# Low half of each weight tile from ACT and an accumulating DMA in place of a DVE subtraction (one Trainium2 core, two-layer encoder trunk)

## Chip, cores and metric

One core of one Trainium2 chip. The metric is device time in microseconds (us) of one execution of the whole program; lower is better. Below, PE is TensorE (matmuls), PEld its weight loads, DVE is VectorE, ACT is ScalarE, POOL is GpSimd and SP is SyncE, which here only issues DMAs.

## What is computed

The reference is a two-layer trunk on one sequence of 512 tokens with 1024 features, all in float32. Cut to what matters:

```python
for l in range(DEPTH):                       # DEPTH = 2
    h = rms_norm(x, norm1_g[l])
    za, xb, q, k, v, g = jnp.split(h @ w_in[l], splits, axis=-1)
    ya = spatial_gating(jax.nn.gelu(za), ...)   # A: gMLP gating
    yb = multiscale_pool(xb, ...)               # B: trailing mean pooling
    yc = retention(q, k, v, g, ...)             # C: retention, 8 heads
    x = x + jnp.concatenate([ya, yb, yc], axis=-1) @ w_out[l]
    x = x + conv_ffn(rms_norm(x, norm2_g[l]), w_up[l], ..., w_down[l])   # D_FF = 2816
return rms_norm(x, final_g)
```

## The kernel before, in words

Every large matmul is made to float32 accuracy from three matmuls on float32r operands, a rounded form of float32. An operand a is split into a high half (a rounded to float32r) and a low half (a minus that high half, rounded again), and a product is hi·hi + hi·lo + lo·hi. `mm3` (lines 210 to 214) issues the three for one 128x128 piece of a weight: line 212 (weight hi, activation hi), 213 (weight hi, activation lo), 214 (weight lo, activation hi). So the low half of a weight is first needed by the third matmul.

All weights lie in memory as 192 tiles of 128 partitions by 1024 float32 (512 KB each), 96 a layer, in the order of use. The class `Weights` (lines 54 to 95) brings them in. `first` makes tiles 0 to 3 in halves, interleaved with the loads of x; the change doesn't touch it. The other 188 come from `_emit` (lines 80 to 89): SP issues the load into a raw tile `wr` (line 83), ACT rounds it into the high half `wh` (line 86), DVE subtracts `wh` from `wr` into the low half `wl` (line 87). Each of the three kinds has five buffers. `get(s)` (line 91) is called just before the matmuls of tile s and emits up to tile s + 3 (LOOK = 3). A raw buffer is free for the next load when its readers are done; a `wh` or `wl` buffer is free when the matmuls of its tile are done.

A layer runs in stages. Mixing (lines 246 to 582): the projection v (4 tiles), then the list MIX (lines 43 to 46), with 18 tiles of projections among attention-like work (`scores`, `ymix`), pooling, gating; then the output projection o (8 tiles). In step `q` (lines 321 to 336) POOL issues four SBUF-to-SBUF DMAs of 128 KB that copy half tiles `qs` across partitions, and `scores` (line 353) reads them. Then the FFN in two halves (lines 584 to 629): 22 tiles of up projections, each followed by a short chain on DVE and ACT (lines 604 to 616), then 11 tiles of down projections. That is 22 + 8 + 66 = 96 tiles a layer. The last down projection is laid out by `finish` (line 633) in token halves so that the final norm overlaps it.

Nothing orders the engines by hand: a tile framework works out the waits (semaphores) and plans the order of each engine's queue ahead of time. Each engine then runs its queue strictly in order. The planned order isn't the order of the code. POOL's queue holds a few small memsets, the table loads and the `qs` copies.

Of the kernel before, what the change touches and what calls it, by code (L numbers as in the profile page):

```python
# [10 lines left out]
F32 = mybir.dt.float32  # L11
F32R = mybir.dt.float32r
AF = mybir.ActivationFunctionType
ALU = mybir.AluOpType
# [39 lines left out]
class Weights:  # L54
# [25 lines left out]
    def _emit(self, s):  # L80
        nc = self.nc
        src = self.raw_pool.tile([P, KT, P], F32, tag="raw", name=f"wr{s}")
        nc.sync.dma_start(out=src, in_=self.w[s].rearrange("p (k c) -> p k c", k=KT))
        hi = self.hi_pool.tile([P, KT, P], F32R, tag="hi", name=f"wh{s}")
        lo = self.lo_pool.tile([P, KT, P], F32R, tag="lo", name=f"wl{s}")
        nc.scalar.copy(hi, src)  # L86
        nc.vector.tensor_tensor(out=lo, in0=src, in1=hi.bitcast(F32), op=ALU.subtract)  # L87
        self.slots[s] = (hi, lo)
        self.slots.pop(s - LOOK - 2, None)

# [741 lines left out]
```

## Time and profile before

| what | value |
|---|---|
| time before, median of 2 runs | 1140.86 us (1140.46 and 1141.26) |
| span of the profiled execution, first to last instruction | 1139.3 us |
| what lies around the span, by those two runs | 1.2 to 2.0 us |
| PE busy | 1125.2 us (99%) |
| DVE busy | 746.4 us (66%) |
| ACT busy | 525.1 us (46%) |
| POOL busy | 27.5 us (2%) |
| granted TensorE clock, mean | 0.998 |

The profiled execution has no stopwatch time of its own besides its span, so the two timed runs say what lies around it. A profile line of a group reads: code line, engine, operation, output tile <- input tiles, shapes, count, then busy time in us and mean ns of one, then the engine's idle time before them and what ended it. `xN` is a count. A name ending in q (SPq, ACTq) is the engine's queue, where it waits or issues. PE's matmuls are pipelined: one is listed with 0.39 us but the next starts 0.23 us later.

### The profile page before, as it was taken

How to read it: one execution, taken by the hardware profiler on the slowest of the kernel's cores; microseconds unless marked ns; L12 is line 12 of the kernel's file. 1: busy time of each engine (PE TensorE's matmuls, PEld its weight loads, DVE VectorE, ACT ScalarE, POOL GpSimd, SP SyncE). 2: the span in 40 equal slices, each digit the busy share in tenths (PEclk: the TensorE clock that was granted, in tenths of full speed). 3: DMA queues.
4: the chain of work that ended last, by engine and by line, in shares of the span. 5: the costliest groups of instructions: out<-in, count | busy, mean ns of one | idle time of the engine just before them, and what ended most of it. 6: DMA issues, size and time to landing. Idle time of an engine off the chain costs nothing.

```text
span 1139.3 us, 13715 instructions
## 1 busy us (share of the span) xinstructions
PE 1125.2 (99%) x5378; PEld 941.7 (83%) x5378; DVE 746.4 (66%) x1103; ACT 525.1 (46%) x731; POOL 27.5 (2%) x71
## 2 busy tenths in 40 slices
PE   8999999999999999999999999999999999999997
PEld 6888888888888888888888898888888888888886
DVE  6898676576763377764448877666777435777534
ACT  7577745444431244444327785534444213444420
POOL 2010000000000000000001000000000000000000
PEclk9999999999999999999999999999999999999999
DMA  9433222233223222233224322222232223322202
GB/s 326 146 111 93 75 75 96 90 102 102 93 93 101 103 93 93 97 105 113 93 93 123 100 74 71 78 93 93 96 107 94 93 96 106 95 93 93 93 1 74
DMA packets 33361, 112.83 MB, mean 99 GB/s; under 512 B 4320, under 2 KB 4496, under 8 KB 33296
## 3 DMA queue, kind: packets, MB, share of 16 engines
q1 hardware_dynamic: 29952, 103.82, 27.1%
q0 software_dynamic: 2480, 6.87, 2.3%
q10 hardware_dynamic: 864, 1.26, 0.3%
q8 instruction: 42, 0.69, 0.2%
q14 instruction: 23, 0.19, 0.0%
HBM read 105.64 MB, written 2.10 MB: 95 GB/s over the span
## 4 chain that ended last, share of the span: by engine, by line
PE 99%; DVE 0%; DMA 0%; ACT 0%; issue 0%; DVEq 0%; SPq 0%; ACTq 0%
PE up L214 14%; PE up L212 14%; PE up L213 14%; PE dn L214 5%; PE dn L213 5%; PE dn L212 5%; PE o L212 3%; PE o L214 3%; PE o L213 3%; PE fd L212 2%; PE fd L213 2%; PE fd L214 2%; PE v L241 1%; PE v L242 1%; PE v L243 1%; PE k L213 1%
## 5 line engine op out<-in xcount | busy, mean ns | idle before, releaser
L86 ACT CAST wh<-wr 128x1024 fp32r<-128x1024 f32 x188 | 197.7, 1052 | 291.7 <-PE dn L213 104.2
L87 DVE TENSOR_TENSOR wl<-wr,wh 128x1024 fp32r<-128x1024 f32 x188 | 229.8, 1223 | 106.0 <-ACT wh L86 103.1
L610 DVE SCALAR_TENSOR_TENSOR cc<-uu,vecs,cc 128x511 f32<-128x511 f32 (+1 forms) x176 | 131.4, 748 | 5.4 <-ACT cc L606 2.3
L606 ACT ACTIVATE cc<-uu,vecs 128x512 f32<-128x512 f32 x88 | 71.5, 815 | 7.9 <-DVE uu L604 7.7
L614 ACT ACTIVATE cc<-cc 128x512 f32<-128x512 f32 x44 | 27.8, 632 | 79.0 <-DVE cc L610 79.0
L604 DVE TENSOR_TENSOR uu<-up,n_1bc 128x512 f32<-128x512 f32 x44 | 30.2, 688 | 40.9 <-PE up L214 40.9
L604 DVE TENSOR_TENSOR uu<-up,n_0bc 128x512 f32<-128x512 f32 x44 | 30.2, 688 | 40.9 <-PE up L214 40.9
L626 DVE TENSOR_TENSOR x<-x,dn 128x512 f32<-128x512 f32 x24 | 16.5, 687 | 40.9 <-PE dn L214 40.9
L212 PE MATMUL up<-n_0h,wh 128*128 128x512 f32 x88 | 34.7, 394 | 0.0
L213 PE MATMUL up<-n_0l,wh 128*128 128x512 f32 x88 | 34.3, 390 | 0.0
L214 PE MATMUL up<-n_1h,wl 128*128 128x512 f32 x88 | 34.3, 390 | 0.0
L212 PE MATMUL up<-n_1h,wh 128*128 128x512 f32 x88 | 34.3, 390 | 0.0
L212 PE MATMUL up<-n_3h,wh 128*128 128x512 f32 x88 | 34.3, 390 | 0.0
L214 PE MATMUL up<-n_5h,wl 128*128 128x512 f32 x88 | 34.3, 390 | 0.0
L214 PE MATMUL up<-n_2h,wl 128*128 128x512 f32 x88 | 34.3, 390 | 0.0
L212 PE MATMUL up<-n_7h,wh 128*128 128x512 f32 x88 | 34.3, 390 | 0.0
L213 PE MATMUL up<-n_4l,wh 128*128 128x512 f32 x88 | 34.3, 390 | 0.0
L213 PE MATMUL up<-n_6l,wh 128*128 128x512 f32 x88 | 34.3, 390 | 0.0
L213 PE MATMUL up<-n_5l,wh 128*128 128x512 f32 x88 | 34.3, 390 | 0.0
L214 PE MATMUL up<-n_6h,wl 128*128 128x512 f32 x88 | 34.3, 390 | 0.0
L214 PE MATMUL up<-n_3h,wl 128*128 128x512 f32 x88 | 34.3, 390 | 0.0
L212 PE MATMUL up<-n_4h,wh 128*128 128x512 f32 x88 | 34.3, 390 | 0.0
(959 smaller groups left out, 3058.3 us busy)
## 6 DMA issues: line engine op xcount, KB each, us to landing
wr<-in_wflat_dram SPq DMA_DIRECT2D x188, 512.0 KB, 3.5
wr<-in_wflat_dram SPq DMA_DIRECT2D x8, 256.0 KB, 7.3
x<-in_xT_dram SPq DMA_DIRECT2D x8, 256.0 KB, 7.8
qs_0h<-qs_0h POOLq DMA_DIRECT2D x8, 128.0 KB, 2.3
qs_1h<-qs_1h POOLq DMA_DIRECT2D x8, 128.0 KB, 3.7
qs_0l<-qs_0l POOLq DMA_DIRECT2D x8, 128.0 KB, 3.4
qs_1l<-qs_1l POOLq DMA_DIRECT2D x8, 128.0 KB, 3.8
out_dram<-fin ACTq DMA_DIRECT2D x4, 256.0 KB, 2.2
```

The costliest lines, as they stand in the source:

```text
L86: nc.scalar.copy(hi, src)
L87: nc.vector.tensor_tensor(out=lo, in0=src, in1=hi.bitcast(F32), op=ALU.subtract)
L212: nc.tensor.matmul(ps, hi[:, k, :], xh, start=first, stop=False)
L213: nc.tensor.matmul(ps, hi[:, k, :], xl, start=False, stop=False)
L214: nc.tensor.matmul(ps, lo[:, k, :], xh, start=False, stop=last)
L241: nc.tensor.matmul(o, hs[k][:, bs], hi[:, kk, :], start=k == 0 and b % pack == 0, stop=False)
L242: nc.tensor.matmul(o, hs[k][:, bs], lo[:, kk, :], start=False, stop=False)
L604: nc.vector.tensor_tensor(out=u, in0=ps, in1=nm.bc, op=ALU.mult)
L606: nc.scalar.activation(out=c, in_=u, func=AF.Identity, scale=w[2], bias=vecs[:, vc + C_CB + t : vc + C_CB + t + 1])
L610: nc.vector.scalar_tensor_tensor(out=c[:, d:], in0=u[:, : T - d], scalar=w[2 - d], in1=c[:, d:], op0=ALU.mult, op1=ALU.add)
L614: nc.scalar.activation(out=c, in_=c, func=AF.Silu)
L626: nc.vector.tensor_tensor(out=X[m], in0=X[m], in1=ps, op=ALU.add)
```

## The change

In `_emit` the subtraction on DVE goes. ACT writes the raw tile times -1, rounded to float32r, into the low tile: that is the negated high half. Then a DMA issued by POOL adds the raw tile to it in place (it reads `wr` and `wl` and writes `wl`, all in SBUF). `wl` is then raw minus high, as before.

```diff
@@ Weights._emit
         nc.scalar.copy(hi, src)
-        nc.vector.tensor_tensor(out=lo, in0=src, in1=hi.bitcast(F32), op=ALU.subtract)
+        nc.scalar.activation(out=lo, in_=src, func=AF.Copy, scale=-1.0)
+        nc.gpsimd.dma_start(out=lo, in_=src, accum_op=ALU.add)
         self.slots[s] = (hi, lo)
```

## Rows read from the trace of the kernel before

**Rows 1.** The page's head and busy times of the whole span.
```profile
span 1139.3 us, 13715 instructions
PE 1125.2 (99%) x5378; PEld 941.7 (83%) x5378; DVE 746.4 (66%) x1103; ACT 525.1 (46%) x731; POOL 27.5 (2%) x71
```

**Rows 2.** The chain that ended last, by engine.
```profile
PE 99%; DVE 0%; DMA 0%; ACT 0%; issue 0%; DVEq 0%; SPq 0%; ACTq 0%
```

**Rows 3.** Waits of PE, the two longest: total us, times, longest.
```profile
PE v L241 <- ACT n_0h L176: 5.6, 1, 5.6
PE frb L689 <- DVE fr1r L162: 1.3, 1, 1.3
```

**Rows 4.** Groups of instructions, the two that make the halves.
```profile
L86 ACT CAST wh<-wr 128x1024 fp32r<-128x1024 f32 x188 | 197.7, 1052 | 291.7 <-PE dn L213 104.2 <-PE up L213 66.8 <-PE o L213 39.8
L87 DVE TENSOR_TENSOR wl<-wr,wh 128x1024 fp32r<-128x1024 f32 x188 | 229.8, 1223 | 106.0 <-ACT wh L86 103.1
```

**Rows 5.** Stretches: PE, PEld, DVE, ACT, POOL busy, granted clock, DMA share, GB/s.
```profile
24.00:160.00 136.00, 136.00 (x770) 115.87 (x769) 115.22 (x218) 91.70 (x150) 11.05 (x28) 1.00 0.34 109
...
100.00:130.00 30.00, 30.00 (x195) 27.15 (x194) 22.71 (x49) 25.76 (x46) 2.06 (x4) 1.00 0.29 89
...
206.00:328.00 122.00, 122.00 (x548) 101.32 (x547) 86.26 (x113) 55.45 (x69) 0.00 (x0) 1.00 0.29 96
```

**Rows 6.** PE in order of time, start and length in us: tile starts, FFN.
```profile
300.91 0.39 PE L212 MATMUL up<-n_0h,wh 128*128 128x512 f32 x1
...
306.35 0.39 PE L212 MATMUL up<-n_0h,wh 128*128 128x512 f32 x1
...
328.56 0.39 PE L214 MATMUL dn<-G_0h,wl 128*128 128x512 f32 x1
```

**Rows 7.** ACT in order of time, the same stretch of the FFN.
```profile
304.74 0.63 ACT L614 ACTIVATE cc<-cc 128x512 f32<-128x512 f32 x1 [1.99 <-DVE cc L610]
306.32 1.06 ACT L86 CAST wh<-wr 128x1024 fp32r<-128x1024 f32 x1 [0.95 <-PE up L213]
307.28 0.81 ACT L606 ACTIVATE cc<-uu,vecs 128x512 f32<-128x512 f32 x1
```

**Rows 8.** DVE in order of time, the subtraction that belongs to that cast.
```profile
307.41 1.23 DVE L87 TENSOR_TENSOR wl<-wr,wh 128x1024 fp32r<-128x1024 f32 x1 [0.17 <-ACT wh L86]
```

**Rows 9.** DMA queues (packets, MB, share of 16 engines) and issues (median us to landing).
```profile
q1 hardware_dynamic: 29952, 103.82, 27.1%
q0 software_dynamic: 2480, 6.87, 2.3%
...
wr<-in_wflat_dram SPq DMA_DIRECT2D x188, 512.0 KB, 3.5
...
qs_1l<-qs_1l POOLq DMA_DIRECT2D x8, 128.0 KB, 3.8
...
dmt<-in_dmask_dram POOLq DMA_DIRECT2D x1, 512.0 KB, 7.4
```

**Rows 10.** POOL in order of time: issues at the start and in mixing.
```profile
2.86 0.53 POOL L139 DMA_DIRECT2D dmt<-in_dmask_dram  x1
3.38 0.54 POOL L141 DMA_DIRECT2D dect<-in_vdec_dram  x1
...
65.28 0.52 POOL L335 DMA_DIRECT2D qs_1l<-qs_1l  x1 [0.37 <-issue]
```

**Rows 11.** Waits of SP's queue, the longest.
```profile
SPq L83 <- DVE wl L87: 944.7, 176, 14.1
```

**Rows 12.** ACT in order of time: a table load; the first tile that `_emit` makes.
```profile
1.67 1.28 ACT L75 ACT_TABLE_LOAD   x1 [1.67 <-PEq L820]
...
21.63 1.05 ACT L86 CAST wh<-wr 128x1024 fp32r<-128x1024 f32 x1 [0.18 <-DMA wr<-in_wflat_dram]
```

**Rows 13.** PE in order of time: first low half from `_emit`; second pair's scores.
```profile
31.26 0.39 PE L214 MATMUL q<-n_0h,wl 128*128 128x512 f32 x1
...
73.72 0.39 PE L361 MATMUL sc<-qs_0h,ks 128*128 128x512 f32 x1
```

## The prediction

> **What bounds the kernel now.** I read the page's head first: PE is busy for 1125.2 of 1139.3 us, DVE for 66%, ACT for 46% [rows 1]. The chain that ended last is PE for 99% of the span [rows 2]. The waits of PE say what is left to win: 5.6 us once, for the first activation, and 1.3 us at the very end; between the two PE waits for nothing [rows 3]. The stretches confirm it: in mixing (24 to 160 us) and in the up projections (206 to 328 us) PE is busy all the time at a granted clock of 1.00, which is the 2.4 GHz level [rows 5]. So the kernel is bound by the number of matmuls. An engine that gets lighter gives nothing by itself, and the question is only whether the new way of making the low half is ever late. I therefore looked for how early the low half is made today, and for what the new steps share with others.
>
> **How early it is today.** A tile's 24 matmuls take 306.35 - 300.91 = 5.44 us in the FFN [rows 6]. The cast at 306.32 waited for PE to give back a buffer (the releaser is PE's line 213) [rows 7]; with five buffers this is the tile used four tiles later, at 306.35 + 4 x 5.44 = 328.11, and its low half is first read at 328.56 [rows 6]. The subtraction ends at 307.41 + 1.23 = 308.64 [rows 8]. So the low half lies ready for 19.9 us. It is the five buffers that set this, not the speed of the maker.
>
> **What is removed.** 188 subtractions of 1.223 us, 229.8 us of DVE [rows 4]. They lie beside PE's work and PE never waits for them [rows 3], so their going is worth 0. DVE falls from 746 to 517 us of busy time.
>
> **What is added on ACT.** 188 passes over 128x1024. The trace has no such pass with a factor; the nearest row is the cast of the same tile, 1.052 us [rows 4]. Below I take that as the floor too (the same elements), above the 0.81 us for 128x512 with two vector operands [rows 7], twice: 1.62. I take 1.05, since a constant factor brings no operand from memory. ACT rises to 525 + 188 x 1.05 = 722 us (63%). In the up projections ACT is busy for 55.45 of 122 us, 2.47 us a tile [rows 5]; 2.47 + 1.05 = 3.52 of 5.44, so there it is hidden with room, at the upper price too (4.09). Mixing is tighter: 91.7 of 136 us, with 22 tiles 23 more, 115 (84%), while DVE goes from 115.2 to about 88 [rows 5]; the two change places. The tightest stretch is 100 to 130 us: ACT is busy for 25.76 of 30 us, and with its four tiles it reaches 29.96. Nothing covers an ACT that has no idle time left. From below the cost is 0 (PE had no wait beside a DVE at 85%); from above it is all four passes in each of two layers, 8.4 us. I take one pass a layer, 2.1 us, because those four low halves need not be early and can stand behind more urgent work.
>
> **What is added on POOL and the DMA engines.** 188 issues. POOL issued a DMA of the same 512 KB (dmt) in 0.53 us and the next 0.52 us after it began [rows 10]: 0.53 of 5.44 us, on an engine busy for 2%. Nothing there.
>
> The transfer itself isn't in this trace: no DMA adds. The loads' queue took 27.1% of 16 engines over 1139.3 us for 103.82 MB, that is 4940 engine-us, or 195 ns for 4096 bytes, one partition's row; POOL's queue by the same sum 250 ns [rows 9]. An engine has 8 of a tile's 128 rows, so a load occupies it for 8 x 0.195 = 1.56 us of 5.44, a share of 0.29, which is the share that the stretch shows [rows 5]. An adding row reads two rows and writes one. Below it costs one copy (195 ns, reads and write overlapped), above three in a row (585 ns). I take two, 390 ns, as the middle: two rows must be read through the same engine. A tile then occupies each engine for 3.12 us, with the load 4.68 of 5.44 us, a share of 0.86. It fits. At one copy the share is 0.57; at three it is 6.24 us and doesn't fit (the second rival).
>
> The Trainium skill, page "Collectives: The Full Stack", section "The bandwidth ceiling: the fold count and why AG ≠ RS ≠ AR", says that the adding unit in a DMA engine costs nothing by itself and that a sum runs at half a copy's rate because both sources are read through one ring, with 62.28 against 32.35 GB/s measured. By that price, an estimate, the row costs 1.93 copies, 376 ns, and the share is 0.84. No row here shows an adding DMA.
>
> **Is it late?** From the tile's cast the new path is 1.05 (cast), 1.05 (negation), 0.53 (issue) and the landing. A plain load lands 3.5 us after its issue [rows 9], of which 1.56 are its rows; with 3.12 in their place that is 5.1 us. Together 7.7 us after 306.32, at 314.0, against 328.56: 14.5 us to spare. With the 7.4 us of dmt, the longest 512 KB landing from POOL, it is 12.2. In the FFN and in o the cost is 0. SP's loads change what they wait for: today for the subtraction (944.7 us in 176 waits) [rows 11], then for the adding DMA's landing. A raw buffer comes back some 5 us later, and its next load must land (3.5 us) before the cast five tiles (27.2 us) on: 27.2 - 7.7 - 3.5 leaves 16 us. Also 0.
>
> The one early place without much room is tile 4: cast at 21.63 to 22.68 [rows 12], negation to 23.73 if it stands next, landing 5.6 us later at 29.4; PE reads it at 31.26 [rows 13]. With a landing of 7.4 us in place of 5.1 it comes at 31.7, and behind one more pass of ACT about 1 us later: at most 1.5 us late. I take 0.
>
> **The sum.** 1139.3 (span) + 0 (FFN, o) + 2.1 (mixing) + 0 (start) = 1141.4, and about 1.6 around the span by the two timed runs (1.2 to 2.0): **1143 us**. Its own range is 1138 to 1152 (nothing; all 8.4 in mixing and 1.5 at the start).
>
> **Rivals.**
>
> *POOL's queue delays the copies that scores wait for* (slower). The adding DMAs share POOL's queue with the qs copies. The last copy of the second pair is issued at 65.28 [rows 10], lands 3.8 us later by the median [rows 9], at 69.1, and PE reads that pair at 73.72 [rows 13]: 4.6 us to spare. Two adding DMAs ahead of the copies cost 2 x 3.12 = 6.2 us, 1.6 late; at three copies a row 9.4, 4.8 late. With 8 such sets, 13 to 38 us, in the middle 26: 1139.3 + 26 + 1.6 = 1167. It decides from two adding DMAs ahead. Against it: mixing makes one tile in 6.2 us (136 / 22), so two ahead are rare, and POOL's order is planned ahead, with these transfers in view.
>
> *The DMA engines become the bound* (slower). It decides from a row of (5.44 - 1.56) / 8 = 485 ns on, 2.5 copies. At three copies a tile takes 6.24 us, 0.80 more, for the 148 tiles of o and FFN 118 us, less some 17 us of room used up once a layer: 1139.3 + 84 + 1.6 = 1225; at four copies far more. For it: 0.86 is not far from 1, and POOL's rows cost 250, not 195 ns. Against it: two reads alone make two copies.
>
> *POOL takes the next adding DMA only when the last has landed* (slower). At 7.4 us a tile, 1.96 over, 148 times, less 34: 1397. Against it: at the start POOL issued one after the other in half a microsecond while each landed in some 7 us [rows 9, 10].
>
> *The ACT copy needs another function table* (slower). The pass is an ACTIVATE between Silu and Identity. Two table loads a tile, of 1.28 us [rows 12], would make 2.47 + 1.05 + 2.56 = 6.08 us on ACT, 0.64 over 5.44, in 88 up tiles: 1139.3 + 56 + 1.6 = 1197. Against it: Identity (line 606) and Silu (line 614) take turns without a load between [rows 7]. The Trainium skill, page "ScalarE: Activation LUTs", section "Table sets: the hidden batching unit", says that copy is in every set; by it the rival's price is 0, and the trace agrees for Identity.
>
> *Faster by over 2%.* PE's two longest waits are 6.9 us together [rows 3], 0.6%. Only a tighter matmul could do it, and nothing here points to one.
>
> **How the numbers follow.** About 2% can be told from no change here: 1118.0 and 1163.7. Forecast 0.71, POOL's queue 0.08 (a third of it inside 2%), DMA bound 0.14, waiting for landings 0.04, table 0.02, faster 0.01. So faster 0.01, same 0.74, slower 0.25. The range 1138 to 1180 holds the forecast and the first rival, 0.79.
>
> **What would show it.** Right: PE's only waits are those of rows 3 and a few below 2 us in mixing; DVE near 517, ACT near 722 us; the negation near 1.05 us; POOL's queue with 188 x 128 more row packets at 300 to 450 ns, and DMA share near 0.85 in the up projections; landings of 5 to 8 us. Wrong: PE waiting for `wl` in the FFN with DMA share near 1 (second rival) or below it with issues far apart (third); PE waiting for `sc` behind late qs copies (first); table loads on ACT in the FFN (fourth).

## The result, and the profile after

The changed kernel takes 1148.76 us (median of two runs, 1148.54 and 1148.97) against 1140.86; the ratio on record is 1.0067, with a 95% interval of 1.0049 to 1.0086. It is slower by 7.9 us, inside the 2% and inside the range, and 5.8 us above the forecast of 1143. The profiled execution took 1148.54 us with a span of 1146.8, so 1.7 us lie around the span.

After the change a line number from 88 on stands one higher than in the code before: L87 is the negation on ACT, L88 the adding DMA, L213 to L215 are `mm3`. First the page's head and the busy times of the changed kernel, which answer to [rows 1]:

```profile
span 1146.8 us, 14169 instructions
...
PE 1130.0 (99%) x5378; PEld 941.4 (82%) x5378; DVE 534.4 (47%) x915; ACT 693.1 (60%) x919; POOL 192.8 (17%) x259
```

PE still has 5378 matmuls, yet is busy for 4.8 us more; the first experiment shows where. DVE and ACT have changed places. ACT has exactly 188 instructions more. The chain that ended last, by engine, which was PE for 99% [rows 2]:

```profile
PE 90%; ACT 4%; DMA 3%; DVE 2%; issue 1%; ACTq 0%; DVEq 0%; POOLq 0%; SPq 0%
```

The path now leaves PE at some places and runs through ACT, a DMA and DVE. The groups that make the halves (line, engine, operation, count | busy us, mean ns of one | idle time before, and what ended it):

```profile
L86 ACT CAST wh<-wr 128x1024 fp32r<-128x1024 f32 x188 | 197.4, 1050 | 188.3 <-issue 84.5
L88 POOL DMA_DIRECT2D wl<-wr x188 | 164.6, 876 | 868.6 <-ACT wl L87 815.9
L87 ACT ACTIVATE wl<-wr 128x1024 fp32r<-128x1024 f32 x188 | 197.8, 1053 | 12.3 <-PE v L243 12.3
```

The negation costs what the cast costs. POOL's issue of an adding DMA takes 876 ns. The DMA queues and the issues, in the columns of [rows 9]:

```profile
q0 software_dynamic: 29552, 105.45, 50.3%
q1 hardware_dynamic: 29952, 103.82, 27.4%
...
wr<-in_wflat_dram SPq DMA_DIRECT2D x188, 512.0 KB, 4.6
wl<-wr POOLq DMA_DIRECT2D x188, 512.0 KB, 5.8
...
qs_1l<-qs_1l POOLq DMA_DIRECT2D x8, 128.0 KB, 5.1
```

POOL's queue has taken 0.503 x 16 x 1146.8 = 9229 engine-us, 419 of which it had before (0.023 x 16 x 1139.3). The remaining 8810 over 188 x 128 = 24,064 rows are 366 ns for an adding row, 1.88 times the 195 ns of a loaded one. The Trainium skill, page "Collectives: The Full Stack", section "The bandwidth ceiling: the fold count and why AG ≠ RS ≠ AR", has the sum at 1/1.93 of a copy's rate, measured on a ring between cores. The trace agrees for this transfer inside one core: 1.88. PE's waits (total us, times, longest):

```profile
PE v L242 <- ACT n_0h L177: 6.2, 1, 6.2
...
PE y L382 <- ACT S_2h L122: 0.9, 2, 0.5
...
PE sc L362 <- DVE ks L346: 0.5, 1, 0.5
PE sc L362 <- PE q L215: 0.2, 1, 0.2
```

No wait names `wl`. The new ones are all in mixing and make 1.6 us together, far less than 7.5. So the list of waits doesn't hold the loss, and I compared the two traces matmul by matmul. Six of the changed kernel's matmuls, in order of time (start, length):

```profile
32.13 0.39 PE L215 MATMUL q<-n_0h,wl 128*128 128x512 f32 x1
...
167.55 0.39 PE L213 MATMUL o<-c_2h,wh 128*128 128x512 f32 x1
...
305.43 0.39 PE L213 MATMUL up<-n_0h,wh 128*128 128x512 f32 x1
...
333.08 0.39 PE L215 MATMUL dn<-G_0h,wl 128*128 128x512 f32 x1
...
632.13 0.40 PE L213 MATMUL q<-n_0h,wh 128*128 128x512 f32 x1
...
706.49 0.50 PE L213 MATMUL xb<-n_0h,wh 128*128 128x512 f32 x1
```

The first, third and fourth stand in [rows 13] and [rows 6] for the kernel before; the others there are:

```profile
163.03 0.39 PE L212 MATMUL o<-c_2h,wh 128*128 128x512 f32 x1
...
627.62 0.40 PE L212 MATMUL q<-n_0h,wh 128*128 128x512 f32 x1
...
699.54 0.50 PE L212 MATMUL xb<-n_0h,wh 128*128 128x512 f32 x1
```

The changed kernel is behind by 0.87 us at the start (32.13 - 31.26), by 4.52 after mixing, by 4.52 at both places in the FFN, still by 4.51 where the second layer mixes, and by 6.95 when that is done. So the 7.5 us of span are 0.87 (start) + 3.65 (mixing, layer 0) + 0 (o and FFN) + 2.44 (mixing, layer 1) + 0 (o and FFN) + 0.5 (the last norm and the stores). The start follows the arrival of the first activation, 6.2 for 5.6 us of wait. It wanders: in the runs below the first matmul of `q` lies anywhere from 0.9 us before to 0.6 us behind that of the kernel before, so the 0.87 isn't counted to the change. The 0.5 us at the end isn't either: it is 0 with seven raw buffers and 0.5 with ACT's passes alone.

The stretches of the changed kernel (busy times as in [rows 5]: PE, PEld, DVE, ACT, POOL; granted clock, DMA share, GB/s):

```profile
24.00:160.00 136.00, 134.61 (x743) 112.87 (x743) 88.25 (x190) 107.42 (x167) 29.43 (x48) 1.00 0.76 182
...
206.00:328.00 122.00, 122.00 (x548) 101.25 (x547) 61.26 (x91) 74.53 (x92) 19.22 (x22) 1.00 0.83 190
```

In the up projections PE is as full as before with the DMA engines at 0.83 in place of 0.29. In the window over mixing PE gets through 743 matmuls in the 136 us, 27 fewer than before, at the same granted clock.

### The profile page after: what moved, and what is told of

Read it like the earlier page. It is cut to its first block, busy times and chain, and to the rows that moved or that the text cites. A ratio compares the mean times of both kernels' runs of the same rounds, so it can differ in the third digit from the quotient of the medians.

```text
span 1146.8 us, 14169 instructions
## 1 busy us (share of the span) xinstructions
PE 1130.0 (99%) x5378; PEld 941.4 (82%) x5378; DVE 534.4 (47%) x915; ACT 693.1 (60%) x919; POOL 192.8 (17%) x259
## 4 chain that ended last, share of the span: by engine, by line
PE 90%; ACT 4%; DMA 3%; DVE 2%; issue 1%; ACTq 0%; DVEq 0%; POOLq 0%; SPq 0%
PE up L213 14%; PE up L214 14%; PE up L215 14%; PE dn L214 5%; PE dn L215 5%; PE dn L213 5%; PE o L215 3%; PE o L213 3%; PE o L214 3%; DMA wr<-in_wflat_dram 2%; PE fd L213 2%; PE fd L214 2%; PE fd L215 2%; PE g L214 1%; PE g L213 1%; PE g L215 1%
## 5 line engine op out<-in xcount | busy, mean ns | idle before, releaser
L88 POOL DMA_DIRECT2D wl<-wr x188 | 164.6, 876 | 868.6 <-ACT wl L87 815.9
L87 ACT ACTIVATE wl<-wr 128x1024 fp32r<-128x1024 f32 x188 | 197.8, 1053 | 12.3 <-PE v L243 12.3
L605 DVE TENSOR_TENSOR uu<-up,n_0bc 128x512 f32<-128x512 f32 x44 | 30.2, 688 | 35.8 <-PE up L215 29.2
L213 PE MATMUL up<-n_0h,wh 128*128 128x512 f32 x88 | 34.6, 393 | 0.0
L213 PE MATMUL up<-n_1h,wh 128*128 128x512 f32 x88 | 34.3, 389 | 0.0
L215 PE MATMUL up<-n_0h,wl 128*128 128x512 f32 x88 | 34.3, 389 | 0.0
L213 PE MATMUL up<-n_2h,wh 128*128 128x512 f32 x88 | 34.3, 389 | 0.0
L215 PE MATMUL up<-n_1h,wl 128*128 128x512 f32 x88 | 34.3, 389 | 0.0
L215 PE MATMUL up<-n_2h,wl 128*128 128x512 f32 x88 | 34.2, 389 | 0.0
L213 PE MATMUL up<-n_3h,wh 128*128 128x512 f32 x88 | 34.2, 389 | 0.0
L214 PE MATMUL up<-n_2l,wh 128*128 128x512 f32 x88 | 34.2, 389 | 0.0
L214 PE MATMUL up<-n_3l,wh 128*128 128x512 f32 x88 | 34.2, 389 | 0.0
L215 PE MATMUL up<-n_3h,wl 128*128 128x512 f32 x88 | 34.2, 389 | 0.0
L213 PE MATMUL up<-n_4h,wh 128*128 128x512 f32 x88 | 34.2, 389 | 0.0
```

The source lines that it names most:

```text
L87: nc.scalar.activation(out=lo, in_=src, func=AF.Copy, scale=-1.0)
L88: nc.gpsimd.dma_start(out=lo, in_=src, accum_op=ALU.add)
L213: nc.tensor.matmul(ps, hi[:, k, :], xh, start=first, stop=False)
L214: nc.tensor.matmul(ps, hi[:, k, :], xl, start=False, stop=False)
L215: nc.tensor.matmul(ps, lo[:, k, :], xh, start=False, stop=last)
L605: nc.vector.tensor_tensor(out=u, in0=ps, in1=nm.bc, op=ALU.mult)
```

## The experiments

Four theories run through the expectations. A: ACT's added passes stand among the short steps of mixing that PE's attention matmuls wait for. B: the adding DMA is to blame, by its share of the DMA engines or of POOL's queue. C: any change of the work beside PE (first of all the lighter DVE) makes the planned order of PE's queue a different one, and most orders cost some us. D: the raw buffers come back late, because the load behind one now waits for an adding DMA to land. One expectation adds E: the `qs` copies land later. All ratios are against the kernel before, run on the same chip (medians of 1140.6 to 1141.0 us).

### ACT's passes without the DMA

```diff
         nc.scalar.activation(out=lo, in_=src, func=AF.Copy, scale=-1.0)
-        nc.gpsimd.dma_start(out=lo, in_=src, accum_op=ALU.add)
```

> Leaves out the adding DMA: the low half stays the negated high half, made by ACT; DVE makes no low half. Theory A (the 6 us lost in mixing come from the extra ACT passes that stand in ACT's queue ahead of work that PE waits for): the loss stays, 1146 to 1149 us. Theory B (they come from the adding DMAs, which delay the qs copies and the loads): the loss goes, 1140 to 1142 us.

Measured: 1146.46 us (1146.22 to 1146.76), ratio 1.0047 (1.0034 to 1.0059). Mixing is 2.6 us longer in layer 0 and 2.4 in layer 1, o and FFN are not. So most of the loss is there with ACT's passes and the lighter DVE, and no adding DMA near. How it looks, first ACT of this kernel, in order of time:

```profile
75.11 1.05 ACT L86 CAST wh<-wr 128x1024 fp32r<-128x1024 f32 x1
76.06 0.58 ACT L121 CAST S_2h<-sc 128x512 fp32r<-128x512 f32 x1
76.53 1.07 ACT L87 ACTIVATE wl<-wr 128x1024 fp32r<-128x1024 f32 x1
```

PE of the same kernel, behind that and later in the layer:

```profile
76.69 0.39 PE L381 MATMUL y<-S_2h,vv 128*128 128x256 f32 x1 [0.45 <-ACT S_2h L121]
...
140.63 0.44 PE L381 MATMUL y<-S_1h,vv 128*128 128x384 f32 x1
141.00 0.66 PE L421 MATMUL yb<-ident,yr_0r 128*64 128x128 f32 x8
```

And the kernel before, ACT and PE at the same two places (two views):

```profile
73.79 0.59 ACT L121 CAST S_2h<-sc 128x512 fp32r<-128x512 f32 x1
74.26 1.06 ACT L86 CAST wh<-wr 128x1024 fp32r<-128x1024 f32 x1
```

```profile
138.05 0.34 PE L381 MATMUL y<-S_1h,vv 128*128 128x384 f32 x1
138.22 0.33 PE L386 MATMUL y<-S_1l,vv 128*64 128x384 f32 x1
```

Before, the `S_2h` cast stood ahead of the tile's cast; now the plan puts it between the tile's two passes, and PE waits 0.45 us for it. That is the smaller part: 0.9 us of 5.0 in both layers. The plan of PE's own queue has changed too: matmuls of `y` stand singly among groups of `yb`. The same matmul (`y` from `S_1h`) took 0.17 us until the next one began in the kernel before (138.05 to 138.22), and takes 0.37 where a `yb` group follows (140.63 to 141.00); the one step from `y` to a `yb` group that the kernel before had at this place took 0.26. Nobody waits there and PE counts as busy; its busy time has grown by 4.1 us (1129.3 in this kernel, 1125.2 before).

PE's order differs from the old one at three places a layer, and the time is lost just there: 1.1, 0.6 and 0.6 us in layer 0, 1.1, 0.6 and 0.7 in layer 1, together 4.8 of the 5.0 (the waits for `S_2h` are part of the first). The changed kernel and the ones below with seven raw buffers or a later negation have this same order of PE's 5378 matmuls. All five lose 2.40 to 2.44 us in the mixing of layer 1, with the adding DMA or without it. So the loss goes with the order. Whether the order alone would make it, with no passes on ACT, no run shows.

### The new way in o and FFN alone

```diff
+        if s % SLOTS_PER_LAYER < 26:
+            nc.vector.tensor_tensor(out=lo, in0=src, in1=hi.bitcast(F32), op=ALU.subtract)
+        else:
+            nc.scalar.activation(out=lo, in_=src, func=AF.Copy, scale=-1.0)
+            nc.gpsimd.dma_start(out=lo, in_=src, accum_op=ALU.add)
```

> Tiles 0 to 25 of each layer (v, mixing, the first four of o) by the subtraction on DVE, the other 70 by ACT and the adding DMA. Theories A and B alike, if all of the loss belongs to tiles made during mixing: 1140.5 to 1142 us, with the FFN as long as before. A loss of more than 2 us would mean that the new way costs something in the FFN or at the stage borders too.

The first four tiles of o, which are made while mixing still runs, keep the old way too.

Measured: 1141.20 us (11 runs, 1140.27 to 1142.14), ratio 1.0002 (0.9993 to 1.0011). Its stretches:

```profile
24.00:160.00 136.00, 136.00 (x770) 115.75 (x769) 115.85 (x219) 92.32 (x152) 11.08 (x28) 1.00 0.35 109
...
206.00:328.00 122.00, 122.00 (x548) 101.25 (x547) 62.02 (x92) 74.91 (x92) 19.18 (x22) 1.00 0.84 192
```

PE's order in mixing is the old one, matmul for matmul, and the loss is gone while o and FFN make their low halves the new way at a DMA share of 0.84. So the whole loss belongs to the tiles made during the mixing of a layer, and the price of nothing for the FFN and the other four tiles of o is shown by a run.

### The negation on DVE, the adding DMA kept

```diff
-        nc.scalar.activation(out=lo, in_=src, func=AF.Copy, scale=-1.0)
+        nc.vector.tensor_scalar(out=lo, in0=src, scalar1=-1.0, scalar2=None, op0=ALU.mult)
```

> The negation is made by DVE in place of ACT, the adding DMA stays; ACT has the work of before and DVE one pass a tile, as before. Theory A: the loss goes, 1140 to 1143 us. Theory B: it stays, 1146 to 1149 us. Both: DMA share near 0.83 in the up projections, as in the changed kernel.

Measured: 1148.88 us (1145.69 to 1149.09), ratio 1.0062 (1.0049 to 1.0075). The pass takes 687 ns on DVE, where the subtraction took 1223 [rows 4]. Two of PE's waits in the profiled execution:

```profile
PE sc L362 <- DVE ks L346: 0.9, 1, 0.9
...
PE sc L363 <- DMA qs_0l<-qs_0l: 0.5, 1, 0.5
```

With ACT as it was, the kernel still loses, 1.9 us of it at the first pair's scores (53.5 us into the span). So there is a part that comes with the DMA: B or D, not A. Another 2.7 us go elsewhere in the mixing of both layers, 0.8 of them in waits for `ysq` from ACT, under an order of PE's queue that differs from the old one and from that of the changed kernel. So a loss of this size doesn't need ACT's passes; C may have a share here. The profiled execution was the fastest one (1145.69); the others lie near 1148.9 at a granted clock of 0.995 for 0.997. What adds those 3.2 us was not profiled and stays open; 0.002 of clock over 1147 us would be 2.3 us, an estimate from those two figures.

### Two raw buffers more

The place to look at is ahead of the first scores. ACT of the changed kernel:

```profile
39.78 1.05 ACT L86 CAST wh<-wr 128x1024 fp32r<-128x1024 f32 x1 [5.07 <-DMA wr<-in_wflat_dram]
```

The same cast in the kernel before:

```profile
37.19 1.05 ACT L86 CAST wh<-wr 128x1024 fp32r<-128x1024 f32 x1 [3.35 <-PE q L213]
```

And PE of the changed kernel:

```profile
55.04 0.50 PE L362 MATMUL sc<-qs_0h,ks 128*128 128x512 f32 x1 [0.52 <-DVE ks L346]
```

ACT stands for 5.07 us for a load. In the kernel before, the same cast waited for PE, not for a load; so the load is late, ACT's next steps are late, and 15 us on PE waits for `ks`. The tile is number 9. Its load goes into the raw buffer of tile 4 and was issued at 31.23, just behind the landing of tile 4's adding DMA at 31.17; in the kernel before it was issued at 24.00. It then took 8.5 us to land, where the median is 4.6 and the same load took 4.3 before: four more adding DMAs were issued from 27.07 to 33.00. With 4.6 us it would have landed at 35.8, by this estimate in time. So the late buffer (D) and the crowded DMA engines (B) make this wait together.

```diff
-        self.raw_pool = ctx.enter_context(tc.tile_pool(name="wraw", bufs=5))
+        self.raw_pool = ctx.enter_context(tc.tile_pool(name="wraw", bufs=7))
```

> The changed kernel with seven raw buffers in place of five. Theory D (the adding DMA's part of the loss comes from raw buffers that come back late, so that early in mixing ACT stands 5 us waiting for a load and the first pair's scores come 0.8 us late): that part goes, some 1 us, 1146.5 to 1148 us, with no wait of ACT for a load at 35 to 40 us. Theory E (it comes from the qs copies that land later): unchanged, 1148 to 1149.5 us. Both leave the 5 us that the run with ACT alone showed.

Measured: 1146.84 us (1146.44 to 1147.27), ratio 1.0054 (1.0042 to 1.0067). Two of PE's waits:

```profile
PE q L215 <- DMA wl<-wr: 1.2, 1, 1.2
PE y L382 <- ACT S_2h L122: 0.9, 2, 0.5
```

The wait for `ks` is gone, and so are the 1.05 us by which layer 0 lost more than the kernel without the DMA (3.65 against 2.6). So seven buffers cure that part, as D says; both counts start at PE's first read of tile 4's low half. A new wait of 1.2 us ends there, at 31.72. The adding DMA isn't slower: it takes 6.6 us from issue to landing, and 6.5 in the changed kernel, where it lands at 31.17 for a read at 32.13. PE is early here: the first matmul of `q` begins 1.8 us sooner than in the changed kernel. What is left of the loss in mixing, 2.5 and 2.4 us, is that of the kernel with ACT's passes alone.

### The negation one tile later, with five and with seven raw buffers

```diff
-        nc.scalar.activation(out=lo, in_=src, func=AF.Copy, scale=-1.0)
-        nc.gpsimd.dma_start(out=lo, in_=src, accum_op=ALU.add)
+        self._low()
+        self.pending = (src, lo)
```

Here `_low` negates and adds the tile before, so that a cast is never followed by its own negation.

> The changed kernel, but negation and adding DMA of a tile are emitted one tile later, so that the planner ranks them behind more of the attention work. Theory A (ACT passes ahead of urgent work): the loss in mixing falls to 3 us or less, 1142 to 1145 us; the FFN keeps its length, since of some 12 us to spare 5.4 go. Theory C (any other plan of PE's queue costs some us, whatever ACT does): 1145 to 1150 us. If the room in the FFN was less than read, PE waits for the low half there and the time is over 1155 us.

> The deferred form with seven raw buffers. Theories A and D together: 1141 to 1143 us, as both parts of the loss go. Theory C: 1145 to 1150 us.

Measured: 1150.98 us (1150.95 to 1151.67), ratio 1.0092 (1.0077 to 1.0108), with five raw buffers; 1147.29 us (1146.93 to 1147.82), ratio 1.0059 (1.0046 to 1.0071), with seven. With five the time lies just above C's range, far above A's; with seven what A and D together had forecast is missed, and C's 1145 to 1150 holds. PE's waits with five:

```profile
PE sc L373 <- DVE ks L357: 2.6, 1, 2.6
PE q L226 <- DMA wl<-wr: 1.5, 1, 1.5
```

With five buffers the raw tile is held still longer, and the wait for `ks` grows from 0.5 to 2.6 us: this speaks for D once more. PE's order is that of the kernel with ACT's passes alone in both, and with seven so are its steps in mixing (2.5 and 2.4 us lost). So where in the code the pass is written doesn't decide where the plan puts it, and this pair doesn't remove A's part as I had expected.

### The negation on POOL

```diff
-        nc.scalar.activation(out=lo, in_=src, func=AF.Copy, scale=-1.0)
+        nc.gpsimd.tensor_scalar(out=lo, in0=src, scalar1=-1.0, scalar2=None, op0=ALU.mult)
```

> The negation is made by POOL, in the same queue as the adding DMA; ACT and DVE are both relieved. Theory A: 1140 to 1143 us, if POOL's pass of 128x1024 takes less than the 5.44 us of a tile less the 0.9 us of an issue. Theory B: 1146 us or more, as the qs copies wait behind POOL's passes as well. If a POOL pass takes over 4.5 us, POOL becomes the bound and the time rises by (pass + 0.9 - 5.44) x 148 us.

Measured: 1151.58 us (1149.15 to 1152.00), ratio 1.0087 (1.0073 to 1.0101). The group, from the page:

```profile
L87 POOL TENSOR_SCALAR wl<-wr 128x1024 fp32r<-128x1024 f32 x188 | 528.2, 2814 | 298.5 <-PE up L215 131.5
```

At 2.8 us the pass is 2.7 times ACT's. PE waits 2.8 us for `ks`, and 1.9 for the scale of a norm (`n_0r`). An idle engine isn't free when its pass is that long: the raw tile is held longer, as in the run before, and POOL's issues and `qs` copies stand behind the passes.

### The adding DMA twice

```diff
         nc.gpsimd.dma_start(out=lo, in_=src, accum_op=ALU.add)
+        nc.gpsimd.dma_start(out=lo, in_=src, accum_op=ALU.add)
```

> A second adding DMA of the same tile behind the first, so the low half is the wrong sum. If the 366 ns that a row occupies its engine are capacity, a tile needs 8 x (0.366 x 2 + 0.195) = 7.4 us of each engine and the DMA engines are the bound: FFN tiles of about 7.4 us, 1141 + 148 x 2.0 + 44 x 1.2 - 34, about 1450 us. If part of the 366 ns is only waiting, FFN tiles of 5.5 to 6.5 us and 1150 to 1300 us.

Measured: 1547.08 us (1546.38 to 1547.78), ratio 1.3563 (1.3538 to 1.3588). Its DMA queues:

```profile
q0 software_dynamic: 56624, 204.03, 72.1%
q1 hardware_dynamic: 29952, 103.82, 18.2%
```

PE in the up projections, at two tiles in a row:

```profile
306.39 0.50 PE L216 MATMUL up<-n_0h,wl 128*128 128x512 f32 x1 [2.31 <-DMA wl<-wr]
...
313.79 0.50 PE L216 MATMUL up<-n_0h,wl 128*128 128x512 f32 x1 [1.67 <-DMA wl<-wr]
```

PE waits for `wl` at nearly every tile (80 waits in 88 up tiles), and the period is 7.40 us here (7.7 and 7.9 at the next two) in place of 5.44. By the sum of the prediction a tile with two adds takes an engine 1.56 + 2 x 8 x 0.366 = 7.42 us, nearly that period; with one add it is 1.56 + 2.93 = 4.49 of 5.44, which fits. But POOL tells of a second thing: the second add on the same tile must wait for the first, and POOL stood 1118.2 us in all for those landings, with the next tile's add behind it. So this kernel mixes the second rival with the third, and the next one takes them apart. The total is above what was expected because PE also falls to half the clock behind many of these waits (mean granted clock 0.933).

### The second add into another tile

```diff
         nc.gpsimd.dma_start(out=lo, in_=src, accum_op=ALU.add)
+        nc.gpsimd.dma_start(out=self.spares[s % 2], in_=src, accum_op=ALU.add)
```

> The changed kernel with a second adding DMA a tile that goes into one of two spare tiles in turn, so that it needn't wait for the first (the spare tiles are read by nothing). With the second add on the same tile the time was 1547, and two things were mixed in it: rows of 7.42 us a tile on each DMA engine, and POOL standing 1118 us for the first add's landing. If the DMA engines set that period, it stays near 7.4 us a tile: 1450 to 1560, DMA share 0.95 or more in the up projections, PE waiting for wl at nearly every tile. If POOL's standing set it, the period falls towards what the engines can do at the shortest rows seen (8 x (0.16 + 2 x 0.327) = 6.5 us): 1350 or less.

Measured: 1580.23 us, one run beside 1140.62 for the kernel before. Its chain that ended last, by engine:

```profile
DMA 72%; PE 13%; issue 5%; ACT 3%; POOL 3%; DVE 1%; SPq 0%; POOLq 0%; DVEq 0%; ACTq 0%
```

The time didn't fall, so POOL's standing for the first add was not what set the period. The transfers did: 72% of the chain (loads 35%, first adds 34%), with both queues together at 72.1 + 18.5 = 90.6% of the engines' time. The first half of layer 0's up projections, which begin at 271.7 us here:

```profile
272.00:443.00 171.00, 139.13 (x544) 109.29 (x543) 61.61 (x91) 74.53 (x91) 38.93 (x44) 0.90 0.95 203
```

The DMA share is the 0.95 that was expected of engines that set the period. The total lies 20 us above the range, and PE's waits in the up projections are fewer and longer (52 of 130.5 us in all, up to 6.0). POOL now stands for loads instead, 1094 us, since a raw tile is held until both its adds have landed and the next load comes behind that. So two adds a tile are too much for the transfers with five raw buffers; whether with more buffers the engines' rows alone would set the limit wasn't tried.

### No low half at all

```diff
-        nc.scalar.activation(out=lo, in_=src, func=AF.Copy, scale=-1.0)
-        nc.gpsimd.dma_start(out=lo, in_=src, accum_op=ALU.add)
-        self.slots[s] = (hi, lo)
+        self.slots[s] = (hi, hi)
```

> From tile 4 on no low half is made at all: no subtraction, no negation, no adding DMA; the matmuls of the low half read the high half. ACT has the work of before, DVE 230 us less, PE the same number of matmuls. Theory A (the 5 us are ACT's extra passes): 1139.5 to 1141.5 us, as ACT is as before. Theory C (the planner orders PE's queue anew when the work beside it changes, and most orders cost some us in mixing): 1142 to 1147 us although there is less to do, with PE's order in mixing other than before.

Measured: 1142.16 us (11 runs, 1141.37 to 1142.81), ratio 1.0010 (1.0002 to 1.0019). Its busy times:

```profile
PE 1126.2 (99%) x5378; PEld 941.5 (83%) x5378; DVE 537.1 (47%) x915; ACT 520.4 (46%) x731; POOL 27.5 (2%) x71
```

DVE is as light as in the changed kernel and ACT as before, and the time is 1.2 us above the kernel before: a lighter DVE gives nothing, and the new plan that comes with it even costs a little. It lies at the lower edge of what C had forecast, with 0.44 us lost in the mixing of each layer under an order of its own. That is the lighter DVE's part with its plan; with ACT's passes it is 5.6 us.

### ACT's passes cut short

As in the run before, without a low half; but ACT negates an eighth of each tile into a spare one.

```diff
         nc.scalar.copy(hi, src)
+        spare = self.spare_pool.tile([P, 1, P], F32R, tag="spare", name=f"wx{s}")
+        nc.scalar.activation(out=spare, in_=src[:, 0:1], func=AF.Copy, scale=-1.0)
         self.slots[s] = (hi, hi)
```

> No low half (its matmuls read the high half, as in the run without any low half, 1142.16), and on ACT the negation cut to an eighth of the tile, into a spare tile that nothing reads: as many instructions of ACT as in the changed kernel, but short ones. If the length of ACT's passes makes the loss (theory A, waits and order both), some 0.15 us a pass leave little of it: 1142 to 1143.5. If it is their number, which alone would give the planned order its new shape: 1145 to 1147, the time with the whole passes (1146.46).

Measured: 1144.08 us (8 runs, 1143.18 to 1145.62), ratio 1.0030 (1.0019 to 1.0041), between the two expectations. A pass takes 309 ns, twice what I had reckoned for it. PE of this kernel, where the kernel with the whole passes had `yb` in groups of 8, 6, 8 and 10:

```profile
139.00 0.66 PE L422 MATMUL yb<-ident,yr_0r 128*64 128x128 f32 x8
...
140.09 1.52 PE L422 MATMUL yb<-ident,yr_0r 128*64 128x128 f32 x22
```

This is the order of the kernel with no passes at all, here and in all of the program, and PE no longer waits for `S_2h`. So the number of ACT's instructions doesn't make the order of the changed kernel. Their length may; but PE doesn't read what these passes make either, and no run has whole passes that nobody reads beside a light DVE. In mixing of layer 0 this kernel loses 1.4 us, 0.5 of it in a wait of `yv` for ACT. In layer 1 it loses 2.9: the profiled execution (1145.22 us) waits 0.73 us there, and 1.4 us later the granted clock falls to half for 3.4 us, from 668.4, which costs 1.7. The remaining 0.45 is what this order cost without any pass. The four runs near 1143.4 have a granted clock of 0.996 to 0.998, the others 0.995.

### ACT's pass beside the subtraction

The kernel before, with ACT's whole pass added into a spare tile that nobody reads.

```diff
         nc.vector.tensor_tensor(out=lo, in0=src, in1=hi.bitcast(F32), op=ALU.subtract)
+        spare = self.spare_pool.tile([P, KT, P], F32R, tag="spare", name=f"wx{s}")
+        nc.scalar.activation(out=spare, in_=src, func=AF.Copy, scale=-1.0)
```

> The kernel before with ACT's negation added, into a spare tile that nobody reads; the subtraction on DVE stays, no adding DMA. Theory A: 1145 to 1148 us, as in the run with ACT alone. Theory C, if it is DVE's missing work that changes the order: 1140.5 to 1142 us with PE's order as before; if ACT's added work changes it too, 1143 us or more with another order. If both engines full cost by their waits (ACT 84% and DVE 85% in mixing), over 1148 us.

Measured: 1166.51 us (1160.60 to 1167.38), ratio 1.0203 (1.0181 to 1.0225). Three stretches of mixing:

```profile
57.70:61.10 3.40, 3.40 (x12) 2.81 (x11) 3.38 (x10) 3.37 (x5) 0.00 (x0) 0.50 0.34 135
115.70:125.90 10.20, 9.32 (x40) 8.93 (x41) 6.95 (x17) 7.77 (x12) 0.52 (x1) 0.50 0.27 88
...
685.70:695.90 10.20, 10.14 (x44) 9.74 (x45) 6.42 (x18) 8.03 (x13) 0.00 (x0) 0.50 0.22 67
```

The same 188 passes cost 5.6 us beside a light DVE and 25.5 beside a full one: now both engines that feed the scores are loaded in mixing, and PE waits 3.4 us for DVE's low halves of the scores, 1.8 for `ks`, and for other tiles. About half of the 25.5 us is the clock: for 3.4 + 10.2 + 10.2 = 23.8 us PE runs at 0.50, the 1.2 GHz level, and does the work of 11.9. The earliest such stretch follows a wait of 1.8 us.

## Why the prediction was right, and where its number was off

The class and the range held, and so did the mechanism in o and FFN: PE bounds the kernel, and their low half is never late. That the loss in mixing lies inside 0 to 8.4 us is partly luck: that bound was worked out from ACT's busy time, while the loss went with PE's order and with a late load, which the working doesn't bound. The steps in order:

- **The sum.** Of the 5.8 us by which 1143 was short, 4.0 lie in mixing (3.65 + 2.44 = 6.1 for 2.1), 0.9 at the start, 0.5 at the end, 0.4 around the span and between the runs. The low end of the range, 1138, doesn't follow from the terms: with nothing in mixing they give 1140.9. And between the two waits of PE in [rows 3] there is one more, 0.6 us in the last norm, which changes nothing.
- **How early the low half is.** Right. After the cast at 310.84 the adding DMA was issued at 314.01 and landed 6.9 us later, at 320.96 (the median is 5.8); PE read it at 333.08, 12.1 us later. The prediction had 14.5, and 12.2 with the longest landing.
- **The adding row.** 390 ns were taken between 195 and 585; it is 366. The DMA share was to be 0.86 in the up projections and is 0.83. The runs with two adds show that the transfers do become the bound, between one add a tile and two; the second rival was real, and the row's price kept it away.
- **ACT's pass.** 1.05 us was taken and 1.053 measured. Busy times came out off by some 20 to 30 us (ACT 693 for 722, DVE 534 for 517). Without any low half DVE has 537, so this is not the DMA: the trace shows neighbours that overlap, as the negation at 311.80 begins before the cast of 310.84 + 1.05 has ended, and the sum of busy times counts such stretches once.
- **"One pass a layer, 2.1 us".** This is the term that was mis-sized. The measured loss is inside its bounds (0 to 8.4), the value was not right: with ACT's passes and the lighter DVE, and no DMA, mixing loses 5.0 us (2.6 + 2.4), and 0.9 with the lighter DVE alone. What was missing is that a pass can cost more than its own length where the plan then puts PE's steps in another order. I had weighed ACT's room, 84% of mixing, and not that PE's queue holds attention matmuls whose order follows what ACT delivers.
- **"Also 0" for the raw buffers.** The working (27.2 - 7.7 - 3.5 leaves 16) was that of the FFN and held there: SP still waits for most of the time and PE never notices. It was used for the whole kernel, and failed at one place in mixing of layer 0, for 1.05 us. There the casts of tiles 4 and 9 are 15.6 us apart in the kernel before (21.63 to 37.19), not 27.2. That alone would leave 4.4 us; but the add was issued 3.5 us after the cast and landed in 6.5, and the load behind it took 8.5, not 3.5. ACT stood 5.07 us for it.
- **The start.** At most 1.5 us late was the bound for tile 4. In the changed kernel nothing is late there, by 1.0 us; in three variants PE waits 0.2, 1.2 and 1.5 us for just that low half.
- **"Their going is worth 0".** True for the kernel as it was (the run without low halves gains nothing). It doesn't hold beside the other edit: with ACT's passes in, DVE's 230 us less are worth 20 us (1166.51 - 1146.46). Two terms that are each priced alone aren't independent when both engines feed one stage.
- **POOL.** 0.53 us an issue was taken from a plain DMA; an adding one takes 0.88. It stays on an engine with 17% and cost nothing.
- **The rivals.** POOL's queue: the landing of the last `qs` copy grew from 3.8 to 5.1 us, and with one add a tile PE waits for a copy only where the negation is on DVE (0.5 us) or on POOL (0.2). With two adds a tile it waits 28 and 55 us for `qs_0h`: the mechanism is there, and with one add far too small. POOL waiting for landings: its wait for ACT ends nearly all of its idle time (815.9 of 868.6 us), none by the landing of an adding DMA. Another function table: ACT has 188 instructions more for 188 passes, so there is no table load; the Trainium skill, page "ScalarE: Activation LUTs", section "Table sets: the hidden batching unit", has copy in every set, and the trace agrees.

What is shown: that o and FFN are free, that the loss is made by the tiles of mixing, that most of it stays with ACT's passes and no DMA, that it goes with one order of PE's queue, whatever the DMA does, that as many short passes don't give this order, and that two more raw buffers take away the part ahead of the first scores. What is argued from rows only: that the order makes the loss, since no run kept the old order with whole passes or had the new one without them, and that the length of the passes makes the order. What is open: the 3.2 us between executions of the kernel with the negation on DVE. No version tried is faster than the kernel before; the one with the old way in mixing equals it.

## What to carry to other kernels

Price a moved step stage by stage, and in a stage where several engines feed TensorE with short steps ask what order a planner will give its queue, not only whether the engine has room: the waits here show 1.6 of 6.1 us. Where a DMA becomes the last reader of a buffer, follow that buffer to its next load at the tightest place, not at the widest. And a bulk step is best placed by stage: with the new way only where PE streams through weights, it costs nothing.

## What the runs showed of the hardware that I had not expected

- The granted clock falls near some short waits and not near others. With the negation a tile later, PE waited 2.58 us before the scores at 57.62, and the trace has it at 0.50 from 57.5 to 60.9 us. With the negation on POOL, 3.4 us at 0.50 begin at 675.3, 1.8 us after a wait of 0.92; but the same run waits 2.78 us before its first scores with the clock at 1.00 behind it. With seven raw buffers a wait of 1.22 us has no such stretch either, nor has the changed kernel, whose longest new wait is 0.52 us. So a wait in mixing can have a second price, some 1.7 us (half of 3.4), that no part of the prediction had; its length alone doesn't tell when.
- An adding DMA between SBUF tiles costs POOL 0.88 us to issue, where a plain one of the same size took 0.53 [rows 10].
- One pass over 128x1024 takes 0.69 us on DVE with a constant, 1.05 on ACT and 2.81 on POOL.
